# adaLN's modulation rows: loaded into the activation store from GpSimd, and summed before the attention

## The chip, the core and the metric

One of the eight cores of a Trainium2 chip runs the whole program; the other cores do nothing. The metric is device time of one launch, in microseconds (us). Engines are named as in the profile: PE (TensorE matmul), PEld (its weight load), DVE (VectorE), ACT (ScalarE), POOL (GpSimd) and SP (SyncE, which only issues transfers). An engine works through its instructions in one fixed order.

## The reference

Two post-norm layers (DEPTH = 2) over 128 context rows and 512 latent rows, 640 in all, width 1024, in fp32. One layer:

```
sh1, sc1, g1, sh2, sc2, g2 = split(silu(cond) @ w_ada + b_ada)   # adaLN, 6 x 1024 columns
z = (x * (1 + sc1) + sh1) @ w_in      # retention q,k,v,g | S5 u | attention q,k,v | 3 x 1024 gates
r = retention(...)                     # 4 heads of 128, both directions
s = gelu(S5 scan of u, both directions);  s = s * sigmoid(s @ w_glu)      # the gated unit
n = neighbourhood attention            # 8 heads of 64
m = (sig(ga) * (r @ wb0) + sig(gb) * (s @ wb1) + sig(gc) * (n @ wb2)) @ w_o
x = layer_norm(ALPHA * x + g1 * m)
f = (gelu(a) * b) @ w_down,  a, b = split(depthwise conv3((x * (1 + sc2) + sh2) @ w_up))
x = layer_norm(ALPHA * x + g2 * f)
```

`cond` has two rows only: one vector for the context rows, one for the latent rows. Outputs are both streams and the context's final states and caches.

## The kernel before

Activations are held transposed (128 channels on the partitions, 640 rows along the free axis). Every fp32 product is made of three matmuls of fp32r operands, hi*hi + hi*lo + lo*hi; so each weight tile is split on arrival: ACT copies it to `hi` (L176) and DVE subtracts to get `lo` (L177).

Work is a list of **units**, made in `layer` and joined in `build`. A unit has `slots` (weight tiles of 128x1024 floats, 512 KB) and an `emit` function. `run` walks the list; it loads slots ahead on SP (`load_to`, L206, a ring `raw` of NRAW = 4 buffers), splits them up to two units ahead into a ring of three `hi`/`lo` pairs, and emits the unit. A projection unit is 48 matmuls of 320 columns (`project`, L148). Beside the units run **generators** (retention, S5, attention), which get `rate` steps per unit of cost. Program order gives priorities; the compiler's planner then lays down each engine's order from estimated times, so an instruction can stand later or earlier than in the program, but never changes place once the program runs.

Intermediates are held in a **store** of NU = 37 buffers of 128x642 floats (`unit`, `free`); a new tile takes the buffer that has been free longest, and waits for its last readers. Attention, S5 and residual rows all live there.

Most of **adaLN** is not a matmul. `ada_rows` takes 128 columns x 1024 of transposed `w_ada` in two halves: each half is one 512 KB load into the `raw` ring (kind "raw", not split), and four DVE multiply-and-sum instructions over 512 elements (L308, each followed by a read of its accumulator) against the two silu vectors `crow`, which `cond_rows` loads and prepares. With the second half come two small adds (L311, L312). Per layer 24 such row units belong to columns 16..40, 8 to columns 40..48, and 16 to columns 0..16 of the next layer. `spread` distributes them over a stretch of the list: columns 16..40 lie from unit ADA[1] = 36 up to the third pair of the attention's query and key projections.

The order in a layer that matters here: S5 input, retention projections (`rg_unit` last), eight gates of branch 0 (`gate_unit`, evacuated by tanh on ACT, L1293), four units of branch 0 (`branch_unit`, evacuated by DVE at L1314, L1310 matmuls), two gated units (`glu_unit`, L1272), then twice a gate of branch 1 and again one, and a branch-1 unit, four times over; then the attention's queries and keys with the `attention` generator, eight gates and four units of branch 2, `w_o`, and the FFN. I call the part from the first gate to the last branch-1 unit the **merge**. S5 in layer 0 is the generator `first_ssm` (rate RATE_S): its recurrence is 64 dependent steps of four DVE instructions (L1193 to L1196); then ACT copies the states (`hs`, L1223) for the output matmuls (L1237, L1239). `ssm_out` reads the result back, applies gelu (L1255) and splits it for the gated units; where the generator isn't through, it is finished there (`need`).

In `attention`, queries and keys of each of four head pairs are split for both heads: four ACT copies for each of two heads (L743, L744, L746, L748) and two DVE subtractions (L745, L747).

Of the kernel before, what the change touches and what calls it, by code (L numbers as in the profile page):

```python
# [10 lines left out]
FT = mybir.dt.float32  # L11
FR = mybir.dt.float32r
I32 = mybir.dt.int32
AF = mybir.ActivationFunctionType
OP = mybir.AluOpType
AX = mybir.AxisListType

P = 128
# [62 lines left out]
class Kernel:  # L81
# [115 lines left out]
    def plan(s, units):  # L197
        s.units, s.cap = units, FIRST
        s.slots = [x for u in units for x in u["slots"]]
        s.raw, s.done, s.nraw, s.nsplit = {}, {}, 0, 0  # L200

    def load_to(s, n):
        while s.nraw < min(n, len(s.slots), s.cap):
# [6 lines left out]
    def split_to(s, n):  # L210
        while s.nsplit < min(n, len(s.slots), s.cap):
            i = s.nsplit
            s.load_to(i + 1)
            t = s.raw.pop(i)
            w = s.slots[i][2]
            if s.slots[i][1] == "raw":
                s.done[i] = (t, None)
            else:
                hi = s.wp.tile([P, 1024], FR, name=s.name("hi"), tag="hi", bufs=NHL)
                lo = s.wp.tile([P, 1024], FR, name=s.name("lo"), tag="lo", bufs=NHL)  # L220
                s.split(hi[:, :w], lo[:, :w], t[:, :w], s.nc.gpsimd if s.slots[i][1] == "pool" else None)
                s.done[i] = (hi, lo)
            s.nsplit += 1

    def run(s, units):
        s.plan(units)
        active, at, held = [], 0, 0
        for u in units:
            n = len(u["slots"])
            s.split_to(at + n)  # L230
            s.load_to(at + n + NRAW - 1)
            for g in u.get("need", ()):
                if g in active:
                    for _ in g[1]:
                        pass
                    active.remove(g)
            tiles = [s.done.pop(at + i) for i in range(n)]
            s.mark(u)
            u["emit"](tiles)
            s.mark(None)  # L240
            at += n
            held += u.get("hold", 0)
            s.split_to(min(at + SPLIT_AHEAD, at + NHL - held))
            s.load_to(at + NRAW)
            active += u.get("start", ())
            for g in list(active):
                g[3] += g[2] * u.get("cost", 0)
                while g[3] >= 1:
                    g[3] -= 1
                    if next(g[1], "end") == "end":  # L250
                        active.remove(g)
                        break
        for g in active:
            for _ in g[1]:
                pass
# [41 lines left out]
    def ada_rows(s, l, m, i, last):  # L297

        def emit(tiles):
            nc = s.nc  # L300
            w = tiles[0][0].rearrange("p (n k) -> p n k", n=2)
            c = slice(2 * m, 2 * m + 2)
            out = s.adac[l][:, c]
            acc = s.small([P, 2, 2], "aacc", 3) if last else out
            junk = s.small([P, 512], "junk", 1, mybir.dt.bfloat16)
            for n in range(2):
                for j in range(2):
                    nc.vector.scalar_tensor_tensor(junk, w[:, n], 1.0, s.crow[j], op0=OP.mult, op1=OP.mult,  # L308
                                                   accum_out=acc[:, n, j:j + 1])
            if last:  # L310
                nc.vector.tensor_tensor(out, out, acc, op=OP.add)  # L311
                nc.vector.tensor_tensor(out, out, s.bcol[l][:, c, None].to_broadcast([P, 2, 2]), op=OP.add)  # L312
                s.ready.add((l, m))
        return dict(slots=[(s.A["w_adaT"][l, m, i], "raw", 1024)], emit=emit)

    def make_gate(s, l, which, half):

# [396 lines left out]
    def attention(s, l):  # L714
        nc, V, G = s.nc, s.nc.vector, s.nc.gpsimd
        for kt4 in range(4):
            hf, i = kt4 // 2, kt4 % 2
            if i == 0:
# [3 lines left out]
                for j in range(4):  # L722
                    x = s.unit([P, 2, 256], base="vb")
# [8 lines left out]
            q, k = s.nq[kt4], s.nk[kt4]  # L732

            kc, own = s.unit([P, 2, 256], base="kc"), [slice(0, 64), slice(64, 128)]
            for e in range(2):
                x = s.A["cache_kT"]
                nc.gpsimd.dma_start(kc[:, e], bass.AP(tensor=x.tensor, offset=x.offset + ((4 * l + kt4) * P + 64 * e) * 256,
                                                    ap=[[0, 2], [256, 64], [1, 256]]))
            qs, kh = ([s.unit([P, T], FR, n) for _ in range(2)] for n in ("qs", "kh"))
            kl = [s.unit([P, T], FR, "kl") for _ in range(2)]  # L740
            kch, kcl = s.unit([P, 2, 256], FR, "kch"), s.unit([P, 2, 256], FR, "kcl")
            for e, r in enumerate(own):
                nc.scalar.activation(qs[e][r], q[r], AF.Copy)  # L743
                nc.scalar.activation(kh[e][r], k[r], AF.Copy)  # L744
                V.tensor_tensor(qs[e][own[1 - e]], q[r], qs[e][r].bitcast(FT), op=OP.subtract)  # L745
                nc.scalar.activation(kh[e][own[1 - e]], kh[e][r].bitcast(FT), AF.Copy)  # L746
                V.tensor_tensor(kl[e][r], k[r], kh[e][r].bitcast(FT), op=OP.subtract)  # L747
                nc.scalar.activation(kl[e][own[1 - e]], kl[e][r].bitcast(FT), AF.Copy)  # L748
            s.split(kch, kcl, kc)
            s.free(q, kc)  # L750
            nbh, held = [], [qs, kh, kl, kch, kcl]
# [5 lines left out]
            for e in range(2):  # L757
# [8 lines left out]
                for ty in range(3):  # L766
                    x = (bt[:, 256 * ty:256 * ty + 256] if ty < 2 else b2).rearrange("p (r c) -> p r c", c=32)
# [44 lines left out]
            for n in range(6):  # L812
                if n < 4:
                    j, bs = n, min(max(16 * n - 8, 0), 32)
                    pp = []
                    for e in range(2):
                        c = slice(LP + 128 * j, LP + 128 * j + 128)
# [33 lines left out]
                if n >= 2:  # L851
                    j = n - 2
# [617 lines left out]
    def layer(s, l):  # L1470
# [93 lines left out]
            add(s.b_unit([A["w_in_b"][l, 2 + hf, i] for i in range(2)], keep_nv(hf)))  # L1564
        for h in range(4):
            add(s.rg_unit(l, h, need=[rets[h]]))
        for c in range(8):
            add(s.gate_unit(l, 0, c))
            if c == 5 and l:
                add(s.action(s.ssm_out, need=[ssm]))  # L1570
        for i in range(4):
            add(s.branch_unit(l, 0, i))
            if i == 1 and not l:
                add(s.action(s.ssm_out, need=[ssm]))
        for i in range(2):
            add(s.glu_unit(l, i))
        for i in range(4):
            for c in (2 * i, 2 * i + 1):
                add(s.gate_unit(l, 1, c))
            add(s.branch_unit(l, 1, i))  # L1580
        c = 0
        for kt4 in range(4):
            add(s.a_unit(s.win(l, 3)[kt4], keep_q(s.nq, kt4)))
            add(s.a_unit(s.win(l, 4)[kt4], keep(s.nk, kt4), start=() if kt4 else [na]))
# [131 lines left out]
    def build(s):  # L1716
        s.adac, s.bcol, s.gate, s.ret, s.ssm, s.ready = {}, {}, {}, {}, {}, set()
        s.rq, s.rk, s.rv, s.rout = {}, {}, {}, {}
        s.nq, s.nk, s.nvd, s.nout = {}, {}, {}, {}
        s.gy, s.sout, s.gts, s.hid, s.chunk = {}, {}, {}, {}, {}  # L1720
        s.preps = [[None, g, r, 0] for g, r in ((s.first_ssm(), RATE_S), (s.ssm_prep(1), RATE_P))]
        s.ada_begin(0)
        s.setup()
        units = [s.hold(s.win(0, 2)[:2])]

        def first(n):
            s.ada_unit(n)
            s.first_h(n)

        for n in range(4):  # L1730
            if n < 3:
                units.append(s.action(lambda n=n: s.ada_load(n + 1), start=[] if n else [s.preps[0]]))
            units.append(s.action(lambda n=n: first(n), cost=1))
        def rest():
            s.free(s.cond)
            s.cap = len(s.slots)

        units.append(s.action(rest))
        def rows(l, a, b, first):

            r = lambda i, last: [s.ada_rows(l, m, i, last) for m in range(a // 2, b // 2)]
            return r(first, False) + [s.action(lambda: s.cond_rows(1 - first))] + r(1 - first, True)

        s.crow = []
        w = len(TURNS)
        done = s.action(lambda: [s.free(s.crow), s.crow.clear()])
        for l in range(s.layers):
            u = [s.action(lambda l=l: s.begin(l))] + s.layer(l)
            find = lambda: [i for i, x in enumerate(u) if x["emit"].__qualname__.endswith("res_unit.<locals>.emit")]
            at = find()  # L1750
            if l + 1 < s.layers:
                extra = [s.action(lambda l=l: s.ada_begin(l + 1))] + rows(l + 1, 0, 16, 0)
                u = s.spread(u, extra, at[w] + 1, at[-w])
            u = s.spread(u, ([s.action(lambda: s.cond_rows(1))] if ADA[2] else []) + rows(l, 40, 48, 1), at[w - 1] + ADA[0], at[w - 1] + ADA[3])
            u = s.spread(u, [s.action(lambda: s.cond_rows(0))] + rows(l, 16, 40, 0) + ([done] if ADA[2] else []), ADA[1], at[0] - 3 - ADA[2])
            u.insert(find()[-w], done)
            units += u
        s.run(units)
# [10 lines left out]

BETWEEN = (0, 0, 0, 8)  # L1770

ADA = (14, 36, 14, 16)

RATE_R, RATE_N, RATE_S, RATE_T, RATE_P = 2.5, 2.75, 1.4, 0.7, 0.5

NU, NRAW, NHL, SPLIT_AHEAD, LEAD = 37, 4, 3, 2, 1


@with_exitstack
# [94 lines left out]
```

## Time and profile before

| | |
|---|---|
| time, median of 3 runs | 2519.05 us (2513.34 to 2520.4) |
| the profiled execution's own time, and its span | 2517.86 us, 2516.1 us |
| busy: PE, PEld | 96%, 93% of the span |
| busy: DVE, ACT, POOL | 71%, 40%, 16% |
| moved from and to HBM | 287 MB, 38 MB: 129 GB/s |
| matmuls at L148 (projections) | 8688 of 17788 |

PE is busy nearly all the time, but "busy" is not full pace: the matmuls are pipelined, and the clock that is granted to PE falls to half in some stretches. Two columns tell that: PEclk (1.00 is 2.4 GHz, 0.50 is 1.2 GHz) and the count of matmuls in a window, which can be compared with that of a window of the same length. An idle time is put down to what ended it ("PE b L1239 <- ACT hs L1223" means that PE's matmul at L1239 started when ACT's `hs` copy was done). The first layer's merge is from 284 to 519 us of the span, the second's from 1540 to 1741 us; attention follows each.

### The profile page before, as it was taken

What the parts mean: (1) busy time and instruction counts of PE and PEld (TensorE: products, weight loads), DVE (VectorE), ACT (ScalarE), POOL (GpSimd) and SP (SyncE); (2) the same over time, 40 slices, a digit from 0 to 9 for tenths busy, and PEclk for the clock granted to TensorE, in tenths of its full rate; (3) what the DMA queues carried; (4) which work ended last, traced back from release to release, by engine and by line L of the source; (5) the groups of instructions that cost most, each with busy time, mean ns of one, the idle gap of its engine ahead of it and who ended that gap; (6) DMA issues with size and microseconds to landing.
All of it is one profiled execution on the core that took longest, in us unless ns stands there. A gap on an engine that the chain in (4) does not pass through costs nothing.

```text
span 2516.1 us, 44967 instructions
## 1 busy us (share of the span) xinstructions
PE 2403.1 (96%) x17788; PEld 2329.7 (93%) x17788; DVE 1774.2 (71%) x4209; ACT 999.9 (40%) x1745; POOL 408.0 (16%) x676
## 2 busy tenths in 40 slices
PE   6999989999999999999999999989999989999996
PEld 3999989998899998999999999989988989999996
DVE  6985846885558888799674577379556888555647
ACT  2365343146633422222335644423664343232231
POOL 4432222013100002110111110420131000000001
PEclk8999979999999999999999999999999999999998
DMA  8853534553233436453444332466233342312322
GB/s 272 267 157 113 168 107 134 180 169 99 66 96 111 130 107 202 141 163 125 139 164 135 97 105 90 147 196 202 71 91 93 109 143 89 96 55 89 93 63 80
DMA packets 108100, 324.19 MB, mean 129 GB/s; under 512 B 24848, under 2 KB 25680, under 8 KB 107888
## 3 DMA queue, kind: packets, MB, share of 16 engines
q1 hardware_dynamic: 62784, 211.32, 26.2%
q0 software_dynamic: 44672, 109.86, 14.6%
q8 instruction: 140, 2.29, 0.4%
q14 instruction: 72, 0.59, 0.1%
q10 hardware_dynamic: 432, 0.13, 0.0%
HBM read 287.09 MB, written 38.21 MB: 129 GB/s over the span
## 4 chain that ended last, share of the span: by engine, by line
PE 58%; issue 22%; DVE 10%; DMA 6%; ACT 3%; POOL 1%; POOLq 0%; DVEq 0%; ACTq 0%
PE pa L148 31%; PE pa L1310 5%; DVE lo L177 2%; DVE junk L308 2%; DMA raw<-in_w_adaT 2%; PE b L1350 2%; PE b L1352 2%; PE b L1351 2%; PE pn L858 2%; DMA raw<-in_w_in_a 1%; PE b L756 1%; PE pa L515 1%; PE pa L517 1%; PE pa L516 1%; PE b L1239 1%
## 5 line engine op out<-in xcount | busy, mean ns | idle before, releaser
L148 PE MATMUL pa<-hth,hi 128*128 128x320 f32 (+2 forms) x2896 | 685.5, 315 | 33.0 <-DVE cv L1394 11.4
L148 PE MATMUL pa<-htl,hi 128*128 128x320 f32 (+2 forms) x2896 | 681.0, 313 | 1.7 <-DVE htl L461 1.0
L148 PE MATMUL pa<-hth,lo 128*128 128x320 f32 (+2 forms) x2896 | 677.7, 312 | 0.4 <-DVE lo L177 0.4
L176 ACT ACTIVATE hi<-raw 128x1024 fp32r<-128x1024 f32 (+1 forms) x316 | 322.4, 1022 | 891.0 <-PE pa L148 335.0
L177 DVE TENSOR_TENSOR lo<-raw,hi 128x1024 fp32r<-128x1024 f32 (+1 forms) x316 | 370.9, 1175 | 272.9 <-ACT hi L176 263.6
L148 PEld LDWEIGHTS pa<-hth,hi 128*128 128x128 f32 x2896 | 490.4, 190 | 49.0 <-issue 15.2
L148 PEld LDWEIGHTS pa<-htl,hi 128*128 128x128 f32 x2896 | 491.8, 189 | 9.2 <-DVE sp_neg L952 1.7
L148 PEld LDWEIGHTS pa<-hth,lo 128*128 128x128 f32 x2896 | 492.0, 190 | 3.1 <-issue 2.1
L308 DVE SCALAR_TENSOR_TENSOR junk<-raw,crow 128x512 bf16<-128x512 f32 x320 | 223.0, 697 | 23.1 <-DMA raw<-in_w_adaT 19.4
L1351 PE MATMUL b<-lo,hdh 128*128 128x256 f32 x784 | 218.0, 281 | 0.0
L1350 PE MATMUL b<-hi,hdh 128*128 128x256 f32 x784 | 215.1, 282 | 2.9 <-ACT hi L176 2.2
L1352 PE MATMUL b<-hi,hdl 128*128 128x256 f32 x784 | 217.3, 281 | 0.0
L1394 DVE SCALAR_TENSOR_TENSOR cv<-pa,conv,cv 128x641 f32<-128x641 f32 (+3 forms) x180 | 153.0, 851 | 5.5 <-ACT cv L1390 3.5
L1350 PEld LDWEIGHTS b<-hi,hdh 128*128 128x128 f32 x784 | 145.8, 188 | 4.8 <-ACT hi L176 3.2
L1351 PEld LDWEIGHTS b<-lo,hdh 128*128 128x128 f32 x784 | 147.6, 188 | 0.2 <-DVE lo L177 0.2
L1352 PEld LDWEIGHTS b<-hi,hdl 128*128 128x128 f32 x784 | 147.2, 188 | 0.0
L1354 DVE TENSOR_TENSOR rm<-b,g 128x256 f32<-128x256 f32 x168 | 69.0, 418 | 74.5 <-PE b L1352 74.1
L515 PE MATMUL pa<-hi,hth 128*128 128x256 f32 x320 | 91.3, 287 | 1.1 <-ACT su L1535 0.6
L516 PE MATMUL pa<-lo,hth 128*128 128x256 f32 x320 | 89.7, 281 | 0.0
L517 PE MATMUL pa<-hi,htl 128*128 128x256 f32 x320 | 89.5, 282 | 0.0
L176 ACT ACTIVATE hdh<-cv 128x641 fp32r<-128x641 f32 x44 | 32.7, 742 | 128.2 <-DVE cv L1402 128.1
L1390 ACT ACTIVATE cv<-pa,conv 128x641 f32<-128x641 f32 (+2 forms) x90 | 76.4, 849 | 17.7 <-PE pa L148 17.7
(440 smaller groups left out, 4370.3 us busy)
## 6 DMA issues: line engine op xcount, KB each, us to landing
raw<-in_w_in_a SPq DMA_DIRECT2D x96, 512.0 KB, 3.8
raw<-in_w_up SPq DMA_DIRECT2D x88, 512.0 KB, 3.6
raw<-in_w_adaT SPq DMA_DIRECT2D x80, 512.0 KB, 4.1
raw<-in_w_down SPq DMA_DIRECT2D x36, 512.0 KB, 3.6
raw<-in_w_branch SPq DMA_DIRECT2D x24, 512.0 KB, 3.6
raw<-in_w_o SPq DMA_DIRECT2D x24, 512.0 KB, 3.7
wada<-in_w_ada SPq DMA_DIRECT2D x32, 256.0 KB, 6.6
raw<-in_w_in_b SPq DMA_DIRECT2D x16, 512.0 KB, 4.7
```

The lines of the kernel that those rows point to most:

```text
L148: s.nc.tensor.matmul(ps[h][:, :n], w[a][:, k], x[b][:, k, c0:c0 + n], start=(k == 0 and part == 0), stop=(k == nk - 1 and part == 2))
L176: s.nc.scalar.activation(hi, src, AF.Copy)
L177: return (eng or s.nc.vector).tensor_tensor(lo, src, hi.bitcast(FT), op=OP.subtract)
L308: nc.vector.scalar_tensor_tensor(junk, w[:, n], 1.0, s.crow[j], op0=OP.mult, op1=OP.mult, accum_out=acc[:, n, j:j + 1])
L515: mm(ps, h[0], x[0], start=(k == 0), stop=False)
L516: mm(ps, h[0], x[1], start=False, stop=False)
L517: mm(ps, h[1], x[0], start=False, stop=(k == 7))
L1310: nc.tensor.matmul(ps[:, h, :n], w[a][:, k, 128 * c:128 * c + 128], out[k][x][:, c0:c0 + n], start=(k == 0 and part == 0), stop=(k == 3 an ...
L1350: mm(ps, a[0], x[0], start=(k == 0), stop=False)
L1351: mm(ps, a[0], x[1], start=False, stop=False)
L1352: mm(ps, a[1], x[0], start=False, stop=(k == nk - 1))
L1394: nc.vector.scalar_tensor_tensor(x[:, o0:o1], z[:, z0:z0 + o1 - o0], cw(tap), x[:, o0:o1], op0=OP.mult, op1=OP.add)
```

## The change

Rows of adaLN no longer go through the `raw` ring. A row unit has no slots but an entry `rows`; `load_rows` takes two 128x512 buffers of the store for it and issues two 256 KB loads from GpSimd's queue. That is done up to ROWS_AHEAD = 2 rows ahead if at least ROOM = 6 buffers are free, else right before the row is summed. Columns 16..40 are now spread from the first gate of branch 0 to the last unit before the attention's projections (27 items over 27 units, one after each unit); `crow` is always freed at their end. Four gates of branch 1 now stand before the gated units, with `ssm_out` in the middle of the four in both layers (it stood after the sixth gate of branch 0 in layer 1, after the second unit of branch 0 in layer 0). RATE_S is 1.25 where it was 1.4. In the attention's split, two of the four ACT copies per head (hi of the queries, second copy of the keys' lo) are DVE copies.

```diff
+        s.rows_in, s.rows_at, s.rows_of = [x for u in units for x in u.get("rows", ())], 0, {}
+    def load_rows(s, n, must):
+        while s.rows_at < min(n, len(s.rows_in)) and (must or len(s.idle) >= ROOM):
+            ts = [s.unit([P, 512], base="arow") for _ in range(2)]
+            for i, t in enumerate(ts):
+                s.nc.gpsimd.dma_start(t, s.rows_in[s.rows_at][:, 512 * i:512 * i + 512])
+            s.rows_of[s.rows_at] = ts
+            s.rows_at += 1
...
     def run(s, units):
...
+            if u.get("rows"):
+                rows += 1
+                s.load_rows(rows, True)
+                tiles = s.rows_of.pop(rows - 1)
...
             s.load_to(at + NRAW)
+            if rows:
+                s.load_rows(rows + ROWS_AHEAD, False)
...
-                    nc.vector.scalar_tensor_tensor(junk, w[:, n], 1.0, s.crow[j], op0=OP.mult, op1=OP.mult,
+                    nc.vector.scalar_tensor_tensor(junk, tiles[n], 1.0, s.crow[j], op0=OP.mult, op1=OP.mult,
                                                    accum_out=acc[:, n, j:j + 1])
+            s.free(tiles)
...
-        return dict(slots=[(s.A["w_adaT"][l, m, i], "raw", 1024)], emit=emit)
+        return dict(slots=[], rows=[s.A["w_adaT"][l, m, i]], emit=emit)
...
             for e, r in enumerate(own):
-                nc.scalar.activation(qs[e][r], q[r], AF.Copy)
+                o = own[1 - e]
                 nc.scalar.activation(kh[e][r], k[r], AF.Copy)
-                V.tensor_tensor(qs[e][own[1 - e]], q[r], qs[e][r].bitcast(FT), op=OP.subtract)
-                nc.scalar.activation(kh[e][own[1 - e]], kh[e][r].bitcast(FT), AF.Copy)
+                V.tensor_copy(qs[e][r], q[r])
+                nc.scalar.activation(kh[e][o], kh[e][r].bitcast(FT), AF.Copy)
+                V.tensor_tensor(qs[e][o], q[r], qs[e][r].bitcast(FT), op=OP.subtract)
                 V.tensor_tensor(kl[e][r], k[r], kh[e][r].bitcast(FT), op=OP.subtract)
-                nc.scalar.activation(kl[e][own[1 - e]], kl[e][r].bitcast(FT), AF.Copy)
+                V.tensor_copy(kl[e][o], kl[e][r].bitcast(FT))
...
+        s.merge_at = len(units) + 1
         for c in range(8):
             add(s.gate_unit(l, 0, c))
-            if c == 5 and l:
-                add(s.action(s.ssm_out, need=[ssm]))
         for i in range(4):
             add(s.branch_unit(l, 0, i))
-            if i == 1 and not l:
+        for c in range(4):
+            if c == 2:
                 add(s.action(s.ssm_out, need=[ssm]))
+            add(s.gate_unit(l, 1, c))
         for i in range(2):
             add(s.glu_unit(l, i))
         for i in range(4):
-            for c in (2 * i, 2 * i + 1):
+            for c in (2 * i, 2 * i + 1) if i > 1 else ():
                 add(s.gate_unit(l, 1, c))
             add(s.branch_unit(l, 1, i))
-        c = 0
+        c, s.na_at = 0, len(units) + 1
...
-            u = s.spread(u, [s.action(lambda: s.cond_rows(0))] + rows(l, 16, 40, 0) + ([done] if ADA[2] else []), ADA[1], at[0] - 3 - ADA[2])
+            u = s.spread(u, [s.action(lambda: s.cond_rows(0))] + rows(l, 16, 40, 0) + [done], s.merge_at, s.na_at)
...
-RATE_R, RATE_N, RATE_S, RATE_T, RATE_P = 2.5, 2.75, 1.4, 0.7, 0.5
+RATE_R, RATE_N, RATE_S, RATE_T, RATE_P = 2.5, 2.75, 1.25, 0.7, 0.5
+ROWS_AHEAD, ROOM = 2, 6
```

## Rows read from the trace of the kernel before

**Rows 1.** Waits of PE over the first merge: what for, total us, times, longest
```profile
PE b L1239 <- ACT hs L1223: 8.9, 2, 7.8
PE pa L148 <- DVE gt L1314: 5.5, 1, 5.5
```
**Rows 2.** Waits of PE over the second merge
```profile
PE pa L148 <- ACT hi L176: 3.3, 1, 3.3
PE pa L1272 <- ACT hi L176: 2.3, 1, 2.3
```
**Rows 3.** Windows: length; busy us (and count) of PE, PEld, DVE, ACT, POOL; clock, DMA, GB/s
```profile
284.10:519.50 235.40, 220.84 (x1444) 219.84 (x1443) 162.06 (x457) 79.40 (x99) 55.26 (x88) 0.91 0.48 150
...
349.20:377.70 28.50, 27.47 (x124) 27.25 (x125) 2.46 (x5) 18.95 (x24) 17.73 (x31) 0.50 0.44 135
377.70:406.20 28.50, 28.50 (x213) 28.50 (x212) 11.84 (x16) 8.52 (x9) 10.32 (x18) 1.00 0.35 102
473.20:480.10 6.90, 5.47 (x20) 5.47 (x21) 6.74 (x15) 1.06 (x1) 0.00 (x0) 0.51 0.47 153
480.10:487.00 6.90, 6.90 (x49) 6.90 (x49) 5.10 (x13) 1.65 (x2) 0.00 (x0) 1.00 0.45 152
...
985.00:992.10 7.10, 3.28 (x12) 3.31 (x13) 7.07 (x13) 2.31 (x3) 0.92 (x2) 0.76 0.74 218
...
1637.90:1644.00 6.10, 3.77 (x16) 3.75 (x16) 6.07 (x13) 2.39 (x3) 0.54 (x1) 0.72 0.55 151
1656.10:1664.50 8.40, 4.72 (x20) 4.46 (x21) 5.04 (x11) 1.65 (x2) 1.14 (x2) 0.80 1.00 220
```
**Rows 4.** Timeline of SP, 440 to 480 us: start us, us, what
```profile
465.93 0.33 SPq L206 DMA_DIRECT2D raw<-in_w_in_a  x1
```
**Rows 5.** Timeline of ACT, 450 to 478 us: idle time before, and its end, in brackets
```profile
470.92 1.06 ACT L176 ACTIVATE hi<-raw 128x1024 fp32r<-128x1024 f32 x1 [7.03 <-DMA raw<-in_w_in_a]
```
**Rows 6.** All waits, 410 to 520 us
```profile
ACT hi L176 <- DMA raw<-in_w_in_a: 32.8, 6, 7.0
```
**Rows 7.** All waits, 1600 to 1741 us
```profile
ACT hi L176 <- DMA raw<-in_w_in_a: 29.8, 7, 5.5
```
**Rows 8.** Groups of DVE, first merge: busy us, mean ns | idle before, releaser
```profile
L308 DVE SCALAR_TENSOR_TENSOR junk<-raw,crow 128x512 bf16<-128x512 f32 x74 | 52.6, 711 | 1.2
...
L308 DVE DVE_READ_ACCUMULATOR junk<-raw,crow 128x1 f32 x74 | 6.0, 81 | 0.0
```
**Rows 9.** Line L1196: duration ns min/median/max, first and last start; then all waits, 280 to 349
```profile
L1196 DVE TENSOR_TENSOR H<-H,rc x56: 218/225/292, 281.0 to 347.5; 128x64 f32<-128x64 f32 x48, 128x128 f32<-128x128 f32 x8
...
DVE lo L177 <- ACT hi L176: 7.7, 9, 1.2
```
**Rows 10.** Timeline of PE, 405 to 416 us
```profile
412.24 0.46 PE L1272 MATMUL pa<-gyhi,hi 128*128 128x320 f32 x2
```
**Rows 11.** Line L308 over the whole span: what ended DVE's idle time before it
```profile
  DMA raw<-in_w_adaT: 19.4, 12
```
**Rows 12.** Timeline of DVE, then of PE, in the first FFN
```profile
981.34 0.69 DVE L308 SCALAR_TENSOR_TENSOR junk<-raw,crow 128x512 bf16<-128x512 f32 x1 [3.85 <-DMA raw<-in_w_adaT]
...
988.82 0.87 PE L148 MATMUL pa<-hth,hi 128*128 128x320 f32 x2 [3.87 <-DVE cv L1394]
```
**Rows 13.** All waits, 2050 to 2060 us
```profile
PE pa L148 <- DVE cv L1394: 2.7, 1, 2.7
```
**Rows 14.** Groups of ACT, 541 to 700 us (attention of the first layer)
```profile
L748 ACT ACTIVATE kl<-kl 64x640 fp32r<-64x640 f32 x6 | 4.4, 734 | 0.1
```
**Rows 15.** Line L395, a DVE copy to fp32r: duration ns min/median/max
```profile
L395 DVE CAST hth<-xT x8: 467/484/908, 21.4 to 62.2; 128x640 fp32r<-128x640 f32 x8
```
**Rows 16.** Window of the first layer's attention, columns as in rows 3
```profile
541.00:700.00 159.00, 153.09 (x1133) 139.63 (x1132) 90.57 (x257) 101.10 (x278) 37.56 (x55) 0.98 0.30 88
```
**Rows 17.** DMA issues: count, KB each, median us to landing
```profile
raw<-in_w_adaT SPq DMA_DIRECT2D x80, 512.0 KB, 4.1
...
x<-in_x_sample POOLq DMA_DIRECT2D x8, 256.0 KB, 4.2
```

More of the change, by code (lines that the diff above doesn't have):

```diff
@@ L215, in split_to @@
             w = s.slots[i][2]
[L216 to L222, printed above, removed]
+            hi = s.wp.tile([P, 1024], FR, name=s.name("hi"), tag="hi", bufs=NHL)
+            lo = s.wp.tile([P, 1024], FR, name=s.name("lo"), tag="lo", bufs=NHL)
+            s.split(hi[:, :w], lo[:, :w], t[:, :w], s.nc.gpsimd if s.slots[i][1] == "pool" else None)
+            s.done[i] = (hi, lo)
             s.nsplit += 1
@@ L226, in run @@
         s.plan(units)
-        active, at, held = [], 0, 0
+        active, at, held, rows = [], 0, 0, 0
         for u in units:
@@ L300, in emit @@
             nc = s.nc
-            w = tiles[0][0].rearrange("p (n k) -> p n k", n=2)
             c = slice(2 * m, 2 * m + 2)
@@ L1753, in build @@
                 u = s.spread(u, extra, at[w] + 1, at[-w])
-            u = s.spread(u, ([s.action(lambda: s.cond_rows(1))] if ADA[2] else []) + rows(l, 40, 48, 1), at[w - 1] + ADA[0], at[w - 1] + ADA[3])
-            u = s.spread(u, [s.action(lambda: s.cond_rows(0))] + rows(l, 16, 40, 0) + ([done] if ADA[2] else []), ADA[1], at[0] - 3 - ADA[2])
+            u = s.spread(u, [s.action(lambda: s.cond_rows(1))] + rows(l, 40, 48, 1), at[w - 1] + ADA[0], at[w - 1] + ADA[1])
+            u = s.spread(u, [s.action(lambda: s.cond_rows(0))] + rows(l, 16, 40, 0) + [done], s.merge_at, s.na_at)
             u.insert(find()[-w], done)
@@ L1770 @@
 BETWEEN = (0, 0, 0, 8)
-ADA = (14, 36, 14, 16)
-RATE_R, RATE_N, RATE_S, RATE_T, RATE_P = 2.5, 2.75, 1.4, 0.7, 0.5
+ADA = (14, 16)
+RATE_R, RATE_N, RATE_S, RATE_T, RATE_P = 2.5, 2.75, 1.25, 0.7, 0.5
 NU, NRAW, NHL, SPLIT_AHEAD, LEAD = 37, 4, 3, 2, 1
+ROWS_AHEAD, ROOM = 2, 6
 @with_exitstack
```

## The prediction

> **What bounds the kernel.** I read the table of busy times first: PE is busy 96% of 2516.1 us, no other engine over 71%. What can be won is PE's idle time and the time in which it runs at half pace. So the next view is PE's waits, stage by stage, and beside them windows with the granted clock and the count of matmuls. The first merge is 235.4 us at a mean clock of 0.91 [rows 3]. Two waits stand in it: 8.9 us for ACT's copy of the S5 state, and 5.5 us for a DVE evacuation [rows 1]. Each is followed by a stretch at half clock: 349 to 378 us shows 124 matmuls at 0.50, the next 28.5 us shows 213 at 1.00; 473 to 480 shows 20 at 0.51, the next 6.9 us shows 49 [rows 3]. So an idle PE is paid for twice, as the wait and then as a clock of 1.2 GHz for some time. The second merge has two waits [rows 2], both in windows below full clock [rows 3].
>
> What lies behind the 5.5 us? The rows share the `raw` ring of four buffers with the weights. SP issues the next weight only when a buffer is free, and a buffer that holds a row is free only when DVE has summed it. The weight of the gate was issued at 465.93 [rows 4], ACT split it at 470.92 after 7.03 us without work [rows 5], DVE's subtraction came after that, and PE stood. ACT waited 32.8 us in six such waits in 110 us of this merge and 29.8 us in seven of the second [rows 6, 7], so weights arrive late as a habit; only a few of the waits reach PE. The DMA engines were half used at 473 (0.47), but full at 1656 (1.00, 220 GB/s) [rows 3].
>
> What lies behind the 8.9 us is the S5 recurrence on DVE, which ends at 347.5 [rows 9]; the S5 output's matmuls wait for it, and they then run in short batches between other engines' work, at half clock.
>
> **The change, term by term**, against the profiled execution's 2517.9 us.
>
> *T1, first merge's ring wait.* With rows out of the ring, SP's four buffers hold weights alone, and DVE's sums stand in no weight's way. The stall's worth: 5.5 us, and in the half-clock window 6.9 - 20/49 x 6.9 = 4.1; the stall reaches about 1.4 us into that window, so 8.2 in all [rows 1, 3]. Bounds 0 (bandwidth was the limit) and -8.2. The half-used DMA engines at that moment speak for the low end; I take -7.
>
> *T2, the S5 output.* Its matmuls move from after the second unit of branch 0 to after the second gate of branch 1: about four projection units later. A generator that starts later finds its recurrence done, so the 8.9 us can go; the half-clock window is worth 28.5 x (1 - 124/213) = 11.9; together 20.8 [rows 1, 3]. Against that: 24 row units now begin with the first gate, each four sums of 0.711 us and four reads of 0.081 us = 3.17 us of DVE [rows 8]. 74 of the 96 sums were in this merge before, so DVE's total there rises by 22 x 0.792 = 17 us, of 162 in 235 [rows 3, 8]. But those sums move to where the recurrence's 56 steps run (four instructions of 0.225 us or 0.29 us each, 51 us in all [rows 9]), of which 7.7 us were idle [rows 9], and can delay it. Moreover the short batches of the S5 output stay short wherever they stand. So the half-clock part need not go. Bounds -20.8 and about +26 (the rival below); I take -4, a fifth of the gain, since planned order and not program order decides it.
>
> *T3, second merge's waits.* By the same cause as T1. 49 matmuls in 6.9 us are 7.1 per us [rows 3]. The two windows: 6.1 - 16/7.1 = 3.8 and 8.4 - 20/7.1 = 5.6, together 9.4 [rows 3]. The second of them is at a full DMA share, and the bytes stay, so part may come back. Bounds 0 and -9.4; I take -7.
>
> *T4, rows in the FFN.* Here DVE itself stood 19.4 us in 12 waits for a row's load [rows 11]. One of them, 3.85 us at 981, is followed directly by PE's 3.87 us at 988.8 [rows 12]; another lies before PE's 2.7 us at 2056 [rows 13]. Two rows loaded ahead on another queue, no longer behind four weights, should be there in time; but with under six idle buffers nothing is loaded ahead, and then each row pays its whole landing of about 4.2 us (such a 256 KB load of POOL [rows 17]) on DVE. The window at 985 is worth 7.1 - 12/7.1 = 5.4 [rows 3], with 2056 it is 8.1. Bounds -8.1 and +8 (the waits double); I take -4. POOL gains two issues per row, 160 in all, and whatever of its own waits for a store buffer delays the rows behind it; POOL is busy 16%, so by itself that is nothing, as long as the rows are ahead.
>
> *T5, attention.* 32 ACT copies (two layers, four pairs, two heads, two copies) of 0.734 us [rows 14], 23.5 us, go; DVE gets 32 copies near 0.48 us [rows 15], 15.4 us. In the first attention ACT is busy 101 and DVE 91 of 159 us, PE 153 at a clock of 0.98 [rows 16]. Neither engine bounds the stage as a whole; nearly equal busy times after the swap (89 and 98) are no worse balanced. 22 of the row sums (17 us) leave the stages behind the merge. Against it, four store buffers are held: after the last row of the merge, two rows of the next group are already loaded, and stay until the first rows in the FFN. Counted from the unit list, 7 to 16 buffers are idle in the attention and 5 to 7 in the `w_o` stage; with four fewer, 3 to 12 and 1 to 3. Bounds -6 (PE's idle time there, 159 - 153) and +20 (a tenth of both attentions' 324 us at half pace would cost 16, plus a stall of 4 for a buffer); I take +1.
>
> *The slower rate* of the first S5 generator (1.25 for 1.4) ends the recurrence later or gives other work room; bounds -4 and +4, half of the 8.9 us that waits for it [rows 1], taken as 0.
>
> Sum: -7 - 4 - 7 - 4 + 1 = -21, so 2496.9. The median of the runs is 1.2 above the profiled execution: **2498**.
>
> A page bears on T4's rows. The Trainium skill, "SBUF — State Buffer", section "SBUF: two separate sides", says that GpSimd writes the descriptors of the transfers that it issues, and that a VectorE copy in a two-port mode locks it out meanwhile, so that the transfer starts late. The trace of before agrees only weakly: POOL's 256 KB loads land in 4.2 us while SP's of 512 KB take 4.1 [rows 17], half the bytes in the same time. This change adds 32 such copies. By that rule T4 would be at its upper end, and the sum 2510.
>
> **Rivals.**
> (a) *Bytes or lateness.* Rows are late on POOL's queue (T4 at +8: 2498 + 12 = 2510), or the bandwidth was the limit in the merges (T1 and T3 at 0: 2512). For: the full DMA share at 1656, and landings of 4.2 us for half the size [rows 3, 17]. Against: 0.47 at the stall of 473 [rows 3]. About 2511, chance 0.13.
>
> (b) *The gain goes in the attention*: four held buffers delay softmax tiles, PE falls to half clock there (T5 at +18): 2498 + 17 = 2515. For: `w_o` has 5 to 7 idle buffers only, and loads wait for the oldest. Against: the attention has the spare ones where it needs them most. Chance 0.14.
>
> (c) *Slower: the rows run ahead of the recurrence.* The planner puts the new row sums before the recurrence's steps on DVE. The place is 284 to 347 us. 15 of the 24 rows stand ahead of the gated unit in the list: 15 x 3.17 = 47.5 us [rows 8]. If all came first, the recurrence would end at 347.5 + 47.5 - 7.7 (the idle time of rows 9) = 387. The gated unit's matmuls began at 412.2, 65 us behind the recurrence's end [rows 9, 10]; they would be ready at 452. PE, with the 20.8 away but four gates of 48 matmuls at 7.1 per us (27 us) put ahead, would get there at 412.2 - 20.8 + 27 = 418, and stand 34 us. T2 is then 34 - 20.8 + 11.9 (the half clock of the output's batches stays) + 4.1 (a stall is followed by half clock, as at 473 [rows 3]) = +29 in place of -4: 2498 + 33 = 2531. The sign turns where T2 is +17, with 12 us less of rows, 36 us, ahead of the recurrence. For: program order gives rows and gates alike early places. Against: the recurrence stands earlier still, and the gates are 27 us of cover. Chance 0.15.
>
> That leaves 0.58 for the forecast, with an own range of 2484 (T1, T3, T4 at their low ends and T2 at half of its gain: -1.2, -2.4, -4.1, -6.4) to 2509 (T2 and T3 at 0: +11). 0.3%, 7.6 us, is about what a measurement can tell here: same is 2511.5 to 2526.6. Of the forecast nearly all is faster; of (a) half; of (b) little: faster 0.65, same 0.20, slower 0.15. The range of 8 in 10 is 2478 to 2524: down to T2's 20.8 whole (2481) with some of T5's gain, up to (a) and (b) with a little more, so that (c) and the far low ends are left out.
>
> **What would show it.** T1 and T3: ACT's waits for gate weights fall far below 32.8 and 29.8 us, and the waits of rows 1 and 2 for `gt` and `hi` are gone. T2: PE's wait at L1239 and the clock between 340 and 400; a recurrence that ends after 360 speaks for (c). T4: DVE's waits at L308 by length, and PE's at 988. T5: PE's busy time and clock in both attentions, and DMA issues or POOL waiting for a store buffer. I am wrong if the merges keep their lengths (235 and 201 us), or if the time appears between 541 and 700 or 1760 and 1925 instead.

## The result, and the profile after

The changed kernel takes 2586.84 us (median of 4 runs, 2581.84 to 2590.02) against 2517.19 us before: a ratio of 1.0276, with its 95% interval in brackets [1.0262, 1.0291]. The forecast was 2498 us, with a range of 2478 to 2524; the change is 2.8% slower, outside the range. The profiled execution has a span of 2584.5 us, 68.4 us more than before.

To see where they are, I divide both spans at the same places of the work, the first gate and the last branch-1 unit of each layer (the second layer's first gate begins at 1522.2 us before, not at the 1540 that I gave above as the start of its merge):

| stretch | before, us | after, us | difference |
|---|---|---|---|
| up to the first gate | 284.1 | 280.8 | -3.3 |
| first merge | 235.4 | 257.7 | +22.3 |
| attention, `w_o`, FFN, next layer's projections | 1002.7 | 1019.4 | +16.7 |
| second merge, from its first gate | 219.3 | 235.5 | +16.2 |
| the rest | 774.6 | 791.1 | +16.5 |

All four long stretches lose. PE's busy share falls from 96% to 94%; the page's first part:

```profile
PE 2429.6 (94%) x17788; PEld 2359.2 (91%) x17788; DVE 1793.0 (69%) x4241; ACT 975.6 (38%) x1713; POOL 499.2 (19%) x836
```

The windows of the changed kernel (columns as in [rows 3]):

```profile
280.80:538.50 257.70, 228.88 (x1467) 224.98 (x1466) 175.60 (x534) 76.88 (x96) 83.79 (x144) 0.87 0.49 155
...
383.50:448.40 64.90, 43.08 (x191) 41.52 (x191) 14.90 (x36) 22.70 (x30) 33.61 (x59) 0.50 0.47 147
...
1677.20:1701.10 23.90, 15.24 (x64) 14.54 (x65) 5.92 (x15) 5.18 (x6) 11.56 (x22) 0.50 0.54 172
```

In the first merge PE now spends 65 us in one stretch at half clock, where before the longest was 34 us, of which [rows 3] shows 28.5. No engine is full there (PE is busy for 43 of the 65 us, POOL for 34), and the DMA engines are half used: a chain of waits. PE's waits in the first merge, then in the second:

```profile
PE b L1251 <- DMA gm<-md: 18.2, 5, 7.7
PE pa L1286 <- ACT gyhi L176: 3.9, 1, 3.9
PE b L1253 <- DMA gm<-gd: 3.6, 2, 1.9
PE b L1253 <- ACT hs L1237: 2.0, 2, 1.5
...
PE b L1251 <- DMA gm<-md: 12.6, 2, 6.8
PE pa L1286 <- ACT gyhi L176: 3.5, 1, 3.5
```

The waits of [rows 1, 2] are nearly all gone: 8.9 us for `hs` is 2.0, the 5.5 us for `gt` and the 5.6 us for weights no longer stand. In their place are PE's waits for `gm`: none in the first merge before, 1.4 us in the second. `gm` are the S5 output's own operands, three tiles for each batch, loaded from GpSimd into buffers of the store. POOL's waits between 340 and 470 us, and its timeline (start, duration, what; idle before it in brackets), show how they come late:

```profile
POOL arow L208 <- PE b L1253: 37.2, 1, 37.2
POOL arow L208 <- ACT gy L1269: 8.9, 2, 5.9
POOL arow L208 <- PE b L1251: 7.0, 1, 7.0
```

```profile
349.88 0.54 POOL L208 DMA_DIRECT2D arow<-in_w_adaT  x1 [5.44 <-DVE rc L1208]
387.58 0.54 POOL L208 DMA_DIRECT2D arow<-in_w_adaT  x1 [37.16 <-PE b L1253]
388.53 2.44 POOL L1258 DMA_DIRECT2D yd<-ym  x4 [0.41 <-DVE ym L1254]
391.42 0.59 POOL L1246 DMA_DIRECT2D gm<-gd  x1 [0.45 <-PE b L1251]
392.00 1.09 POOL L1247 DMA_DIRECT2D gm<-md  x2
...
419.17 0.59 POOL L1246 DMA_DIRECT2D gm<-gd  x1 [5.00 <-PE b L1251]
...
426.28 0.59 POOL L208 DMA_DIRECT2D arow<-in_w_adaT  x1 [2.97 <-ACT gy L1269]
427.91 0.56 POOL L208 DMA_DIRECT2D arow<-in_w_adaT  x1 [1.03 <-DVE gylo L177]
428.47 0.54 POOL L1246 DMA_DIRECT2D gm<-gd  x1
...
430.57 1.07 POOL L1247 DMA_DIRECT2D gm<-md  x2
```

A row's load stands at the head of POOL for 37 us, because the buffer it was given is one that the S5 output reads. That stand looks like the cause, but what is seen behind it was not ready much sooner: the store of the output (`yd`) then waits 0.41 us more for its own data, and the next `gm` load 0.45 us for a buffer. Before, POOL stood nearly as long at the same point, for the output's first result:

```profile
356.74 2.43 POOL L1244 DMA_DIRECT2D yd<-ym  x4 [35.09 <-DVE ym L1240]
```

What differs comes after it. Three `gm` loads are released by PE's reading of an earlier `gm` ("PE b L1251" at 391.42, 406.98 and 419.17 us): load, multiply, free, load, with nothing ahead; three of PE's waits, 3.8, 2.7 and 3.4 us, follow on these. PE's longest wait, 7.7 us to 436.2 us, follows two rows that stood 4.0 us in all for their buffers, directly before its `gm` loads. So buffers and queue both show here.

The two middle rows of the table hold more than the FFN. From the merge's last addition (`mg`, L1336) to the FFN's first evacuation (`cv`), that is in the attention and `w_o`, the first layer takes 287.7 us for 278.4 and the second 285.7 for 273.1: 22 of the 68 us. The windows, before and then after:

```profile
523.70:802.10 278.40, 269.97 (x2034) 254.79 (x2033) 180.59 (x433) 147.42 (x353) 43.98 (x67) 0.99 0.33 100
1745.60:2018.70 273.10, 266.11 (x2033) 251.32 (x2032) 183.36 (x431) 147.06 (x352) 45.19 (x69) 1.00 0.33 101
...
543.20:830.90 287.70, 273.08 (x2039) 257.76 (x2039) 177.36 (x396) 135.62 (x336) 43.69 (x64) 0.98 0.29 86
1798.00:2083.70 285.70, 271.52 (x2039) 256.10 (x2038) 187.45 (x417) 135.49 (x336) 48.12 (x68) 0.98 0.30 90
```

About half of that is lost in the second half of `w_o`, where PE's one wait for an evacuation, 1.3 us before, is 4.8 us in either layer:

```profile
PE pa L1350 <- DVE rm L1354: 1.3, 1, 1.3
...
PE pa L1364 <- DVE rm L1368: 4.8, 1, 4.8
```

In the FFN another operand is late. DVE's waits between 700 and 1330 us before, then between 720 and 1350 us after, in the first layer:

```profile
DVE junk L308 <- DMA raw<-in_w_adaT: 16.0, 10, 3.8
DVE eo L899 <- DMA ebe<-in_b_entry_re: 2.1, 2, 1.9
...
DVE eo L913 <- DMA ebe<-in_b_entry_re: 12.9, 4, 8.3
DVE junk L320 <- DMA arow<-in_w_adaT: 5.3, 5, 2.5
```

The rows themselves arrive better here than before (5.3 us for 16.0), though over the whole kernel DVE waits 22.9 us for them in 15 waits, against the 19.4 of [rows 11]. `ebe`, an operand of the second layer's S5 preparation on the same queue and store, is now late by up to 8.3 us, and DVE's order puts PE's evacuations behind it: PE's wait for `cv` at 1024 us is 6.2 us. That `ebe` was issued late for its own buffer, not behind a row:

```profile
1019.14 0.54 POOL L1082 DMA_DIRECT2D ebe<-in_b_entry_re  x1 [6.91 <-DMA ed<-eo]
```

The stretch from the FFN's first evacuation to the next layer's first gate loses 6.9 us. In the runs below it lies between 5.8 us less and 9.4 us more than before, whatever the buffers, so this loss is not shown to be the store's.

So there were four theories: **Q**, POOL's in-order queue; **S**, the store, whose buffers the rows hold; **P**, the S5 output's new place; and, from the prediction's rival (c), **D**, row sums ahead of the recurrence.

### The profile page after: what moved, and what is told of

Read it like the earlier page. It is cut to its first block, busy times and chain, and to the rows that moved or that the text cites. A ratio compares the mean times of both kernels' runs of the same rounds, so it can differ in the third digit from the quotient of the medians.

```text
span 2584.5 us, 45193 instructions
## 1 busy us (share of the span) xinstructions
PE 2429.6 (94%) x17788; PEld 2359.2 (91%) x17788; DVE 1793.0 (69%) x4241; ACT 975.6 (38%) x1713; POOL 499.2 (19%) x836
## 3 DMA queue, kind: packets, MB, share of 16 engines
q0 software_dynamic: 57472, 151.81, 19.4%
## 5 line engine op out<-in xcount | busy, mean ns | idle before, releaser
L148 PE MATMUL pa<-hth,hi 128*128 128x320 f32 (+2 forms) x2896 | 685.9, 316 | 30.6 <-DVE cv L1408 19.4
L320 DVE SCALAR_TENSOR_TENSOR junk<-arow,crow 128x512 bf16<-128x512 f32 x320 | 219.7, 687 | 25.8 <-DMA arow<-in_w_adaT 22.9
L208 POOL DMA_DIRECT2D arow<-in_w_adaT x160 | 87.3, 547 | 453.4 <-PE b L1253 81.0
```

The costliest lines, as they stand in the source:

```text
L148: s.nc.tensor.matmul(ps[h][:, :n], w[a][:, k], x[b][:, k, c0:c0 + n], start=(k == 0 and part == 0), stop=(k == nk - 1 and part == 2))
L208: s.nc.gpsimd.dma_start(t, s.rows_in[s.rows_at][:, 512 * i:512 * i + 512])
L320: nc.vector.scalar_tensor_tensor(junk, tiles[n], 1.0, s.crow[j], op0=OP.mult, op1=OP.mult, accum_out=acc[:, n, j:j + 1])
```

## Experiments: queue, store, order

After each expectation stand the run's median and its ratio to the kernel before, which ran beside it and took 2516.0 to 2518.6 us. So times of different runs can be compared to some 3 us.

*Rows in the raw ring, the rest of the change kept.*

```
...
-        return dict(slots=[], rows=[s.A["w_adaT"][l, m, i]], emit=emit)
+        return dict(slots=[(s.A["w_adaT"][l, m, i], "raw", 1024)], emit=emit)
```

> Three theories for the 69 us that the change costs. Q: POOL's queue is in order, a row's load waits there for a store buffer, and the S5 output's own loads (gm) and stores (yd) stand behind it, so PE gets its operands late. P: the new place of the S5 output, two gates ahead of the gated unit, leaves its chain of transfers too little cover. D: 17 us more of row sums in the merge hold DVE up. This kernel has all of the change but the carrier: rows go through the raw ring on SP again, at the new places. Q expects PE's waits for gm gone in both merges, 2500 to 2530 us. P and D expect them and the half clock of 383 to 448 us to stay, 2560 us or more.

2525.36 us, 1.0033 [1.0019, 1.0047]. The carrier alone is some 60 of the 69 us; no wait for `gm` is left.

*The old order with the new carrier.*

```
         for c in range(8):
             add(s.gate_unit(l, 0, c))
+            if c == 5 and l:
+                add(s.action(s.ssm_out, need=[ssm]))
         for i in range(4):
             add(s.branch_unit(l, 0, i))
-
-        for c in range(4):
-            if c == 2:
+            if i == 1 and not l:
                 add(s.action(s.ssm_out, need=[ssm]))
-            add(s.gate_unit(l, 1, c))
...
-            for c in (2 * i, 2 * i + 1) if i > 1 else ():
+            for c in (2 * i, 2 * i + 1):
```

> All of the change but the order: the S5 output and the branch-1 gates at the places of the kernel before, rows by POOL into the store. Q expects that rows still stand ahead of the S5 output's loads on POOL, 2550 us or more. P expects both merges back at their old lengths, about 2540 us. D expects no change against the changed kernel, 2580 us.

2612.56 us, 1.0385 [1.0367, 1.0402]: worse than the change. P falls: the new order helps.

*Rows on SP, still in the store.*

```
-                s.nc.gpsimd.dma_start(t, s.rows_in[s.rows_at][:, 512 * i:512 * i + 512])
+                s.nc.sync.dma_start(t, s.rows_in[s.rows_at][:, 512 * i:512 * i + 512])
```

> The changed kernel with the rows' loads issued from SP, still into the store. Q expects PE's waits for gm gone, but a row that waits for a store buffer now holds up the weights behind it on SP: 2510 to 2560 us. P and D expect both merges as in the changed kernel, 2575 us or more. If a lack of idle store buffers alone were the cause (S), whatever the queue, the time would stay above 2570 us as well.

2557.8 us, 1.0166 [1.0151, 1.0181]. The time is in Q's interval, but not for Q's reason. PE's waits in the first merge:

```profile
PE b L1251 <- DMA gm<-md: 16.1, 4, 6.1
```

No row stands on POOL any more, and in the first merge `gm` is about as late as in the changed kernel (18.2). So the store must count. But S alone, which expected more than 2570 us, missed too: in the second merge PE's wait for these `gm` falls from 12.6 to 3.0 us, so where the rows are queued counts as well, or the order that the planner then lays down. P and D missed.

*A ring of four buffers of its own for the rows*, one ahead, NU 34.

```
-            ts = [s.unit([P, 512], base="arow") for _ in range(2)]
+            ts = [s.wp.tile([P, 512], FT, name=s.name("arow"), tag="arow", bufs=4) for _ in range(2)]
...
-NU, NRAW, NHL, SPLIT_AHEAD, LEAD = 37, 4, 3, 2, 1
+NU, NRAW, NHL, SPLIT_AHEAD, LEAD = 34, 4, 3, 2, 1
-ROWS_AHEAD, ROOM = 2, 6
+ROWS_AHEAD, ROOM = 1, 6
```

> The changed kernel with the rows in a ring of four 128x512 buffers of their own, one row ahead; the store has 34 buffers for it in place of 37. Loads stay on POOL. Q expects a row to wait only for DVE's sums of an earlier row, so POOL is held for shorter times: 2520 to 2555 us. P and D expect 2575 us or more.

2551.95 us, 1.0142 [1.0124, 1.0161]: within Q's interval too, but three buffers fewer in the store confound it.

*The store alone: rows in the raw ring, as in the first run, and NU = 33 for 37.*

> The earlier run with rows in the raw ring again took 2525 us, so the carrier is worth some 60 of the 69 us; with the rows on SP but still in the store 28 of them went and PE still waited 16 us for gm in the first merge. So the store may count beside POOL's queue. This kernel is the one with rows in the raw ring, with a store of 33 buffers in place of 37: as many fewer as two rows loaded ahead hold. S (the store: gm tiles get a buffer only when an earlier gm tile has been read by PE) expects the waits for gm in the merges to come back, 2545 to 2565 us. Q alone (POOL's queue) expects no change, 2520 to 2530 us.

2581.62 us, 1.0258 [1.0243, 1.0274]: 56 us for four buffers, without a row on POOL or in the store; more than I expected. The waits for `gm` are back (first merge):

```profile
PE b L1257 <- ACT hs L1241: 11.2, 2, 10.2
PE b L1255 <- DMA gm<-md: 9.2, 2, 5.9
```

The merges are not the main part here, though. Between the two profiled executions with rows in the ring (NU 37 and 33) the merges differ by 15 us (the first by 2.5 only), the attention and `w_o` by 23, and the part ahead of the first gate by 15.

*No row ahead.*

```
-ROWS_AHEAD, ROOM = 2, 6
+ROWS_AHEAD, ROOM = 2, 99
```

> The changed kernel with ROOM = 99: no row is ever loaded ahead of its place, so it holds two buffers in place of four to six, but every row's load is still on POOL. S expects both merges shorter by half of their loss, 2560 us or less in all, with some more waits of DVE for rows in the FFN. Q alone expects as many rows on POOL's queue and the same waits, 2575 to 2600 us.

2522.58 us, 1.0025 [1.0016, 1.0035]: 64 us back from one constant, with every row still on POOL, so Q alone falls. Between the profiled executions of the changed kernel and of this one 40 us lie in the two merges, 22 in the attention and `w_o`, and 4 elsewhere. The dose between:

*Two buffers held in place of four* (ROWS_AHEAD, ROOM = 1, 6), *and two fewer with rows in the ring* (NU = 35).

> The changed kernel with one row ahead in place of two: two store buffers held between rows in place of four. If the loss follows the number of buffers held (S, graded), the time lies between none ahead (2523 us) and two ahead (2587 us), 2540 to 2575 us. If any row ahead on POOL's queue brings the whole loss (Q), it is 2575 us or more.

> Rows in the raw ring, a store of 35 buffers: 37 took 2525 us and 33 took 2582 us. S, graded, expects 2540 to 2570 us. If there is a cliff, it stands near one of the two ends.

2540.38 us (1.0094 [1.0077, 1.0111]) and 2542.64 us (1.0106 [1.009, 1.0122]). Both ways two buffers cost about 17 us, four about 60: graded, steeper toward the end. Counted from the list of units, the fewest idle buffers during the gated unit are 10 in the first merge before, 4 with none ahead, 2 in these two, 0 in the changed kernel and with NU 33. So the new order alone takes six of the ten, and four buffers for rows the rest. Inside the attention's units the fewest are 4 before and with none ahead, 2 in these two, and 0 in the changed kernel and with NU 33.

*A higher threshold* (ROWS_AHEAD, ROOM = 2, 12).

> The changed kernel with ROOM = 12: a row is loaded ahead only where 12 buffers are idle. S expects that none is held over the merge's tight part, and that the time is as with no row ahead, 2515 to 2530 us. If a few rows ahead already hurt, or the FFN's do, it lies between, 2530 to 2570 us.

2573.22 us, 1.0228 [1.0213, 1.0244]: missed. The list explains it: at most units of the merge 12 or more buffers are idle when the row is loaded, and the row is then held into the gated unit, where the count falls to 2, and into the attention, where it falls to 0. So the count in the gated unit does not set the time by itself: with 2 there, one row ahead took 2540 us. A threshold that looks at the moment of loading does not protect a later moment.

*No row ahead, rows on SP* (ROOM = 99 and `nc.sync`).

> No row ahead, the rows' loads on SP in place of POOL (2523 us on POOL). If POOL's queue has a part of its own, SP gives some of it back: 2505 to 2517 us. If the store was all, it is the same within 6 us, or slower by the weights that now wait behind rows on SP: 2520 us or more.

2511.74 us, 0.998 [0.9969, 0.999]: 11 us less, as Q expects of POOL's queue. The planner's order differs too, so how much of it is the queue is not shown.

## Experiments: the rows' place, the rate, the copies

Rows in the ring still cost 8 us, all in the first merge. The recurrence on DVE ends there at 392.7 us, in the changed kernel at 379.3, before at 347.5 [rows 9]. The line of the changed kernel (durations in ns, first and last start in us, from 280 us on):

```profile
L1210 DVE TENSOR_TENSOR H<-H,rc x59: 218/225/293, 283.8 to 379.3; 128x64 f32<-128x64 f32 x48, 128x128 f32<-128x128 f32 x11
```

*RATE_S back at 1.4, rows in the ring at the new places.*

> Rows in the raw ring and all the rest of the change, which cost 8 us against the kernel before, all of it in the first merge, where the recurrence ended at 393 us and not at 348; here with RATE_S back at 1.4. If the slower generator (R) is the cause, the recurrence ends near 350 us and the time is 2512 to 2518 us. If the row sums placed among its steps (D) are, it ends near 390 us still and the time is 2522 to 2528 us.

2551.69 us, 1.0143 [1.0124, 1.0162]; both intervals missed. The recurrence ends at 374.2: the rate makes 18 of the 45 us by which it was late, the rest stays (D). But PE's order now has the S5 output before that and waits:

```profile
PE b L1257 <- ACT hs L1241: 44.1, 2, 43.1
```

The slower rate was what kept PE's order behind the late recurrence.

*Old order, rows in the ring at the new places.*

> Rows in the raw ring at their new places, with the S5 output and the branch-1 gates at their old places. With the rows in the store the old order was 26 us worse than the new one. If the new order by itself helps, this is slower than the 2525 us of the run with the new order, 2535 us or more. If the new order only helped against the rows in the store, this is 2515 to 2525 us, and the recurrence's end decides the first merge.

2572.09 us, 1.0226 [1.0203, 1.0249]: the new order is worth 47 us once the rows are early. It is the cover that the prediction set against rival (c): the gates that now stand before the gated unit.

*Rows at the places of the kernel before, in the ring, and then on POOL with none ahead.*

```
-            u = s.spread(u, [s.action(lambda: s.cond_rows(0))] + rows(l, 16, 40, 0) + [done], s.merge_at, s.na_at)
+            u = s.spread(u, [s.action(lambda: s.cond_rows(0))] + rows(l, 16, 40, 0) + [done], 36, at[0] - 3 - 14)
```

> Rows in the raw ring and at the places of the kernel before (from unit 36 on, the last of them in the attention), with the new order, RATE_S 1.25 and the attention's copies. D (the row sums now stand among the recurrence's steps on DVE and make it late) expects the recurrence's end at 360 us or earlier in place of 393, and 2505 to 2518 us. If the rate or the order makes it late, it ends at 380 us or later and the time is 2520 us or more.

> All of the change, but no row is loaded ahead (ROOM = 99) and the rows keep the places of the kernel before. S and D together expect a store that is free for the S5 output and a recurrence that ends by 360 us: 2500 to 2515 us, faster than both kernels. If rows without the ring are late for their sums there, 2520 us or more, with waits of DVE for rows.

2501.92 us (0.9945 [0.9929, 0.9962]) and 2494.87 us (0.9913 [0.9898, 0.9928]): 23 and 28 us less than with the rows early, and both faster than before, and somewhat below what D, and S with D, expected. The recurrence ends at 349.4 and 353.4. In the second kernel the merges run at a mean clock of 0.98 and 1.00; its windows, then PE's longest waits in the first merge:

```profile
282.60:500.50 217.90, 210.80 (x1475) 207.88 (x1474) 153.27 (x443) 78.97 (x99) 74.16 (x130) 0.98 0.55 170
1502.90:1707.50 204.60, 204.26 (x1439) 203.81 (x1438) 145.35 (x378) 76.32 (x91) 64.35 (x111) 1.00 0.53 168
```

```profile
PE pa L1324 <- ACT glt L1290: 4.1, 2, 2.7
PE pa L1324 <- ACT sohi L1295: 2.0, 1, 2.0
```

17.5 us of the first merge and 14.7 of the second are won against 235.4 and 219.3.

*On that kernel: RATE_S 1.4; rows on SP; the attention's copies back on ACT.*

> None ahead, rows at their old places, RATE_S back at 1.4 (2495 us at 1.25). If the rate mattered only because rows held the recurrence up, this is within 5 us, 2490 to 2500 us. If the rate has its own price with the new order, PE waits tens of us for the S5 state again and it is 2510 us or more.

> None ahead, rows at the places of the kernel before (2495 us on POOL), with the rows' loads on SP. If POOL's queue has its part here too, 2480 to 2490 us. If SP's weights now wait behind rows, or the queue's part went with the early rows, 2493 us or more.

> None ahead, rows at the places of the kernel before (2495 us), and the attention's 32 copies back on ScalarE. The copies alone were worth 0 to 2 us against the kernel before; so 2492 to 2500 us is expected. If VectorE's 15 us matter once row sums stand in the attention too, this is faster, 2485 to 2490 us.

2513.62 us (0.9983 [0.9967, 0.9999]), 2500.75 us (0.9933 [0.9914, 0.9951]) and 2496.48 us (0.992 [0.9901, 0.9938]). The rate has a price of its own, some 18 us: PE waits 7.85 us for `hs` at 340 us again, as in [rows 1], not the tens of us that I expected. SP gives nothing back here, as if the queue's part went with the early rows. The copies are worth nothing either way, as also on the kernel before with their hunk alone:

> The kernel before with nothing changed but the attention's copies: 32 of them on VectorE in place of ScalarE. If they are worth what the prediction took, the time is within 6 us of before, 2511 to 2523 us, with both attentions' lengths within 3 us. If they take VectorE's time on the path, it is 2525 us or more.

2513.87 us, 0.9992 [0.9983, 1.0002].

## Why the prediction was wrong

**T1 and T3, right in mechanism.** With the rows out of the ring, ACT waits for no gate weight any more in either merge: of the 32.8 and 29.8 us of [rows 6, 7], for `in_w_in_a`, nothing is left, and PE's waits for `gt` and `hi` of [rows 1, 2] are gone. The gain cannot be read in the changed kernel, since both merges lose more; the kernel with none ahead and rows late has it, with T2's, in 17.5 and 14.7 us.

**T2, half right.** The S5 output's wait did go (8.9 to 2.0 us), thanks to the gates and the slower rate, and rival (c)'s delay of the recurrence did come: 379 us, where (c) had 387 for the worst case. The new place covers the delay. But the half clock became longer, 65 us, for a reason not in the term: the output's operands. The early rows cost 23 to 28 us, about (c)'s price of 33, though by another way than the gated unit standing.

**T5 is the step that failed**: "four store buffers are held". I took it at +1, and it measured about 60 us: 64 by none ahead, 56 by NU 33. Two things were wrong in it. First, in the stages that I did count, the attention and `w_o`, I set the loss near zero because buffers seemed to be left, counting 7 to 16 and 5 to 7 idle ones between units. Inside the attention's units the fewest are 4, and with the four buffers held 0. These stages lost 9.3 and 12.6 us, 22 in all. That is just above my own bound of +20 and close to rival (b), which took it at +18 with a chance of 0.14. But (b)'s path, half clock in the attention, is not what the windows show: their clock fell only from 0.99 and 1.00 to 0.98. Second, I did not count the merges, which I had down as a gain. Most of the rest lies there, 40 us against none ahead. `gm` lives short there and is loaded from memory, so a buffer fewer is a load less in flight.

**T4, failed for a neighbour.** "POOL is busy 16%, so by itself that is nothing, as long as the rows are ahead": I asked whether POOL would be late for the rows, and not what else takes its buffers from the same store, or is queued behind a row that waits for one. The rows' waits in the first layer's FFN fell from 16.0 to 5.3 us; `ebe`'s, 12.9 us, took their place. Moving the rows from POOL to SP gave 11 us with none ahead, 29 with two ahead (2586.84 against 2557.8), and nothing with the rows late; since SP also changes the planner's order, the queue's own part in these is not shown.

**The rate**, taken as 0 within 4 us, is worth some 18 to 27 us with the new order. **The copies**: 0, as taken; DVE paid more for them than the 0.48 us of [rows 15]:

```profile
L758 DVE CAST qs<-nq 64x640 fp32r<-64x640 f32 x6 | 3.9, 653 | 5.7 <-PE pn L872 5.2 <-PE b L859 0.4
L762 DVE CAST kl<-kl 64x640 fp32r<-64x640 f32 x6 | 3.1, 509 | 0.2
```

**The page's rule.** Rival (a) had rows late on POOL, from the 4.2 us of [rows 17]; those are eight loads of `x` alone, and in the changed kernel the same eight land in 3.2 us. The rows land in 3.4 us:

```profile
arow<-in_w_adaT POOLq DMA_DIRECT2D x160, 256.0 KB, 3.4
```

The Trainium skill, "SBUF — State Buffer", section "SBUF: two separate sides", would have them held up by VectorE's copies. The median shows no sign of it: with none ahead and the rows late they land in 3.5 us with the 32 copies on VectorE and in 3.6 us with them back on ScalarE. What held POOL is named in its waits: buffers.

What stays open: how the 60 us divide between the store and the queue inside the changed kernel, and by what path NU 33 loses 15 us ahead of the first gate. Every run also lets the planner lay out a new order, so differences of some 10 us between two kernels may be its choice and not the edit's.

## What to carry to other kernels

Before a transfer is moved into a shared store, count the idle buffers at every stage between its load and its last reader, inside the units as well as between them, the short-lived tiles' stages first, and write beside the transfer what is queued behind it on its new issuer when its buffer is not free. A look-ahead is paid in buffers of that stage; here none ahead was 64 us better than two. When work is moved in front of a serial chain on the same engine, look at where the chain ends in the trace and not at the sum of busy times.

## What was not expected of the hardware

Late operands cost far more than their waits: in the first merge PE's waits for `gm` add up to 22 us (18.2 + 3.6), but the granted clock stayed at 0.50 for 65 us, through the batches between the waits too; in the kernel with none ahead and the rows late, which has no wait for `gm`, the merge's mean clock is 0.98. Waits for `gm` are not the only way there: the kernel before had none in this merge, and its output's short batches still stood at 0.50 for 34 us.
